# Four 128-column products on four column strips for the last four sections of the modulation

## The chip, the cores and the metric

One core of one Trainium2 chip runs the whole program once. The metric is the device time of one execution in microseconds (us). The engines are named as in the profile: PE is TensorE's matmul side, PEld its weight loads, DVE is VectorE, ACT is ScalarE, POOL is GpSimd, SP is SyncE, which here only issues DMAs.

## What is computed

Two layers share all weights: one for 128 prompt tokens, one for 512 sample tokens, 1024 channels each. Cut to what matters:

```python
mod = silu(cond) @ w_ada + b_ada                      # cond: c_ctx (prompt) or c (sample); 6 x 1024 columns
shift1, scale1, gate1, shift2, scale2, gate2 = split(mod, 6)
h = rms_norm(x) * (1 + scale1) + shift1
P = h @ w_in
mixed = concat(rwkv(P), fnet(P), pool(P))             # rwkv: a delta-rule scan, 8 heads of 64, both directions
x = x + gate1 * (mixed @ w_out)
h = rms_norm(x) * (1 + scale2) + shift2
x = x + gate2 * (relu(h @ w_ff1)**2 @ w_ff2)
y = rms_norm(x)
```

The two condition vectors make the modulation a product of a 2-row matrix with w_ada (1024 x 6144, float32). Sections 0 and 1 (shift1, scale1) are needed before the first projection; sections 2, 4, 3 and 5 (gate1, scale2, shift2, gate2) only behind the mixers.

## The kernel before, in words

All 640 tokens are handled as one [128, 640] row of columns per block of 128 channels. The program runs in three parts.

`first` (line 716) computes the first norm, sections 1 and 0 of the modulation and the projections that the first head pair needs; its order is written out by hand. In it `biasing` (line 813) multiplies the shift with raw blocks of w_in: per block of 128 columns eight products of a [128, 32] stationary operand (`shp`) with 128 moving columns, on the four column strips in turn.

`run_groups` (line 1364) is the part of the mixers. The scan is cut into 24 groups of chunks (4 head pairs, 2 directions, 3 groups each); each group is a generator of stages (products on PE, small masks and copies on DVE, ACT and POOL, at last a chain over the chunks that must follow that of the group before it). At most three groups have a slot. A planner keeps a clock (class `Clock`, line 161) with an estimated cost of each instruction, traces next what comes next by that clock, and `pin` (line 282) makes each compute engine issue in exactly the traced order. Beside the groups there are queues of generators: `preps`, `aux`, `side` and `slow` for background work on the other engines, and `gemms` for products that may fill PE. Lines 1449 to 1457 choose between the next stage of a group and a filler:

```python
a = min(able, key=lambda a: max(a.ready, now + q_.EPS))
gap = a.ready - now
if gap > q_.GAP and gemms and gemms[0].ready <= now + q_.GE:
    gemm_step()          # one step of the first generator of gemms
    continue
if gap > q_.DGAP:
    mm(pm()[:, 0:q_.DN], lm2[:, 0:P], lm2[:, 0:q_.DN], ...)   # a product that nobody reads
```

`gemms` holds first `in_rest` (line 1013, the remaining projections). When that has ended, `second` (line 1560) appends `ada_steps` (line 387) for sections 2, 4, 3, 5, and puts FNet, pooling and `prepare_out` (line 1522, x to channel-major) one behind the other on `slow`. At the end of `prepare_out` the generator `out_half` (line 1505, half of the products with w_out) goes to `gemms`. What is left of all queues is stepped in turn when the last group has ended (line 1476). Then come the rest of w_out, the second norm, the feed-forward and the final norm (lines 1582 to 1730), a dense stream of products with 320 moving columns.

`ada_steps` as `second` uses it handles 512 columns of w_ada at a time, one block of 128 rows a step (`nk` = 1): a DMA on SP brings [128, 1, 512] (256 KB) into one of six slots, three steps ahead (`AH`), and the step issues one product, `sil` [128, 32] stationary (two columns of it are not zero), 512 moving columns, into 32 rows of a PSUM bank: column strip kb % 4 (line 411). Eight steps fill a bank: each strip has the sum over two of the eight row blocks. Then DVE copies the bank (`asb`), four transposes on PE turn it, and DVE adds the four strips and the bias into `mod`. There are 64 product steps and 8 such ends. A float32 product stands in the trace as two matmul records.

Of the kernel before, what the change touches and what calls it, by code (L numbers as in the profile page):

```python
# [13 lines left out]
F32 = mybir.dt.float32  # L14
# [6 lines left out]
P = 128  # L21
D = 1024
# [138 lines left out]
class Clock:  # L161
    """estimate of when each engine and each tile is done with what has been traced; chooses what is traced next"""
# [12 lines left out]
    def cost(self, e, name, out, a, k):  # L175
        n = math.prod(out.shape[1:])
        if e == "P":
            if name == "transpose":
                return 55.0
            x = a[1]  # L180
            if x.dtype != F32:
                return n / 2.4 + (0.5 if x.dtype == F32R else 1.0)
            if out.shape[0] > 64:
                return max(211.0, n / 0.6 + 5.0)
            return 79.0 if n <= 64 else 133.0 * n / 128
        if k.get("op") == ALU.pow:
            return 165.0 * n
        if e == "S" and name == "activation":
            return 145.0 + 0.83 * n
        if e == "V" and name in ("tensor_scalar", "scalar_tensor_tensor") and a[0].space != PSUM and len(a) < 4:  # L190
            return 68.0 + 0.52 * n
        if e == "G" and name != "tensor_tensor":
            return 160.0 + 0.83 * n
        return self.FIXED[e] + self.RATE[e] * n

    def tile(self, x):
        """name of the tile; a new one waits for the last use of the tile whose place it takes"""
        t = x.tensor
        n = t.name
        if n not in self.done:  # L200
            self.done[n] = self.used[n] = 0.0, "P"
            m = getattr(t, "tag_meta", None)
            if m is not None:
                q = self.slots.setdefault(t.cap_key, [])
                q.append(n)
                b = t.bufs or m.bufs
                if len(q) > b:
                    self.done[n] = self.used[q[-1 - b]]
        return n
# [26 lines left out]
class Timed:  # L236
    """an engine whose instructions are noted on the clock"""
# [15 lines left out]
class Task:  # L253
# [4 lines left out]
    def step(self):  # L258
        """one step; it may yield the time that passes before the next, or the tile that the next reads first"""
        c = self.clock  # L260
        c.end = self.ready
        self.state = next(self.gen, "end")
        self.ready = c.end + RD
        if isinstance(self.state, (int, float)):
            self.ready += self.state
        elif hasattr(self.state, "tensor"):
            self.ready = c.done[self.state.tensor.name][0] + RD
        return self.state != "end"


def build(nc, tc, T):
# [10 lines left out]
    def pin(start):  # L282
        """the compute engines issue what was traced since start in the order of the program"""
        prev = {}
        for i in nc.cur_bb.bb.instructions[start:]:
            if i.engine in ENGS:
                if i.engine in prev:
                    tc.add_manual_dep(i, prev[i.engine], mybir.DependencyInfo(mybir.DependencyClass.NoSync, mybir.DependencyReason.DATA),
                                      reason="program order")
                prev[i.engine] = i.name  # L290
# [7 lines left out]
    def pm():  # L298
        return psb.tile([P, 512], F32, tag="b", name="pb")

# [18 lines left out]
    def wsplit(src, c0, hf, lo_eng, raw=None, to=None):  # L319
        """half of the rows of a block of 128 columns"""  # L320
# [9 lines left out]
    def gemm_steps(pss, w, a, kb, first, last, extra=0):  # L330
        """the products of one block of rows, as a generator over the matrix products"""
# [19 lines left out]
    def gemm(src, c0, a, lo_eng, halves=(0, 1), extra=0):  # L351
        """[P, NT] product with a block of 128 columns of the weights: two banks"""
# [32 lines left out]
    mod = cp.tile([P, 48, 2], F32, name="mod")  # L385

    def ada_steps(ks, slots, nk, ahead, queue=None):
        """sections of the modulation: 1024 columns each, 512 at a time; slots name the places of the weights"""
        todo = [(k, h, k2) for k in ks for h in range(2) for k2 in range(KB // nk)]
        place = {}  # L390

        def load(n):
            if queue is None and n < len(todo):
                k, h, k2 = todo[n]
                pool, tag, bufs = slots[n % len(slots)]
                place[n] = pool.tile([P, nk, 512], F32, tag=tag, name="wa", bufs=bufs)
                c0 = k * D + 512 * h
                dma(place[n][:], T["w_ada"][nk * k2 * P:nk * (k2 + 1) * P, c0:c0 + 512].rearrange("(a p) n -> p a n", p=P))

        for n in range(ahead):  # L400
            load(n)
        for n, (k, h, k2) in enumerate(todo):
            load(n + ahead)
            r = place.pop(n) if queue is None else queue.pop(0)
# [11 lines left out]
            yield  # L416
            ps2 = pm()
# [77 lines left out]
    npad = [0]  # L495

    def evac(pss, pp, o=0, b=None):
        """out of the banks, with the bias b, or that of the last two columns; pads between the segments if o is not None"""
# [24 lines left out]
    def proj(pool, pss, mi, out, b=None):  # L523
        """w_in block with centred shift, into out [P, NT]"""
        pp = padded(pool)
        evac(pss, pp, b=b)
        shift_a(mi, pp, out, V)
        shift_b(mi, pp, out, out)
# [13 lines left out]
    def cp(out, ps):  # L542
        """out of PSUM, by the engine that is done with it first"""
# [8 lines left out]
    def mm2(lhsT, rhs):  # L552
        """[P, NT] product in two banks; yields (columns, psum)"""
# [72 lines left out]
    def pool_mix(fp):  # L626
# [12 lines left out]
        for pb in range(2):  # L639
# [6 lines left out]
            def doubling(shape, n, src, sl, tag):  # L646
                """centred window sums along a zero-padded axis: the tiles of half the widest window and of the widest"""
# [46 lines left out]
    def rsq_bcast(sq, op0, s1, op1, s2):  # L694
        """(head sums of sq [P, NT], op0 s1, op1 s2) ** -0.5, spread over the channels of each head: (columns, psum)"""
# [20 lines left out]
    def first():  # L716
        """the first norm, the modulation and the projections that the first groups need"""
        with tc.tile_pool(name="pq", bufs=1) as pq:
# [37 lines left out]
            ada = ada_steps((1, 0), None, 2, 0, wa)  # L756
# [8 lines left out]
            def mids(*plan):  # L765
                """gaps of products, and a step of the modulation behind each"""
# [46 lines left out]
            def biasing():  # L813
                """the products of the shift with the raw weights of the first blocks, as a generator"""
# [44 lines left out]
            def products(n, mid=iter(())):  # L859
                """the n-th half; the weights of the next are split ahead"""  # L860
# [111 lines left out]
    def make_sets(pool, n, tag):  # L972
        """tiles with blocks that stay zero, a set for each slot"""
# [27 lines left out]
    def step(q):  # L1001
        """one step of the first task of a queue"""
# [10 lines left out]
    def in_rest():  # L1013
        """the remaining projections; weights are split half a block ahead of the product"""
# [58 lines left out]
    def prep(c, d, g, pool, out):  # L1073
        """elementwise operands of the chunks of a group"""
# [75 lines left out]
    def group(c, d, g, pool, own, pc, AR, BK):  # L1150
        """chunks g of direction d of a head pair, as a generator over stages"""
# [18 lines left out]
        # ---- Gram blocks, token-major copies  # L1170
# [25 lines left out]
        # ---- inverse of I - T: doubling in 16 bit, one correction step with a float32 residual  # L1196
# [5 lines left out]
        def diag(lhs, rhs, o=0):  # L1202
            """products of the pairs of blocks on the diagonal with the chunks of a pair"""
# [10 lines left out]
        # M V  # L1214
# [49 lines left out]
        # ---- W, Z  # L1264
# [18 lines left out]
        # ---- chain over chunks  # L1283
# [80 lines left out]
    def run_groups(todo):  # L1364
        """todo: (j, g, d) in order; as many in flight as there are slots; the chains of a direction run in order"""
# [24 lines left out]
        while todo or active or prepared or preps:  # L1390
# [17 lines left out]
            # ---- background steps whose operands are there  # L1408
# [96 lines left out]
    def out_half():  # L1505
        """the products of w_out with the channels of the FNet and pooling mixers"""
# [15 lines left out]
    def prepare_out():  # L1522
        """x to channel-major, FNet and pooling outputs split"""
# [36 lines left out]
    def second():  # L1560
        acs.close()
        gemms.append(task(ada_steps((2, 4, 3, 5), [(wp, "whi", WB), (wp, "wlo", WB)], 1, AH)))
# [19 lines left out]
    with tc.tile_pool(name="fc", bufs=1) as fc:  # L1582
# [47 lines left out]
        with tc.tile_pool(name="ffp", bufs=1) as ffp:  # L1630
# [21 lines left out]
            # ---- the last quarter by tokens, and the final norm behind it  # L1652
            with tc.tile_pool(name="op", bufs=2) as op:
# [6 lines left out]
                def part(t, q):  # L1660
                    """half of the channels of a tile of tokens, and the sum of their squares"""
# [108 lines left out]
```

## Time and profile before

| what | value |
|---|---|
| runs of the kernel before | 1136.89, 1140.99, 1140.12 us; median 1140.12 |
| the profiled execution, span from first to last instruction | 1140.2 us |
| mean granted TensorE clock | 0.983 |
| PE busy | 1095.3 us (96%), 9516 instructions |
| DVE, ACT, POOL busy | 544.5, 506.4, 383.3 us |
| modulation products (tile wa) | 192 matmul records, first at 15.4 us, last at 541.4 us |
| DMA of w_ada in the part of the mixers | 64 issues of 256 KB, median 3.2 us to landing |

The page is read from the top: PE is busy nearly all the time, but a busy PE is not a PE at its peak, since a matmul's record covers its latency. The part of the mixers lies between 80 and about 620 us, and there the other engines are busy for half of the time or more; behind it DVE, ACT and POOL fall off and PE runs alone. A start in a row is counted from the start of the span. In the timeline a row merges neighbouring instructions of one kind: its time runs from the first start to the last end, and the next row's start may lie before that end.

### The profile page before, as it was taken

The page shows a single profiled execution, that of the slowest core. Times are in us where ns is not written, and L with a number is a line of the kernel's source. Part 1 is how long each engine was busy: PE and PEld are TensorE (multiplying, and loading weights), DVE is VectorE, ACT ScalarE, POOL GpSimd, SP SyncE. Part 2 cuts the span into 40 slices and gives each one's busy share as a digit, 9 for nine tenths or more (in the row PEclk, how much of TensorE's full clock was granted, in tenths as well). Part 3 has the DMA queues.
Part 4 walks back from the last instruction along what each step waited for, and adds up shares of the span by engine and source line. Part 5 has one row for each costly group of instructions (what it writes and reads, how often), then busy time and mean ns, then how long its engine had stood idle before and what let it go on. Part 6 is the DMA issues. An engine that isn't in the chain of part 4 may idle for free.

```text
span 1140.2 us, 23679 instructions
## 1 busy us (share of the span) xinstructions
PE 1095.3 (96%) x9516; PEld 949.0 (83%) x9516; DVE 544.5 (48%) x1297; ACT 506.4 (44%) x1221; POOL 383.3 (34%) x462
## 2 busy tenths in 40 slices
PE   5999999999999998998999999999999999999996
PEld 3688888788785665565677999999999999999996
DVE  6266665466665654667754664311331233123313
ACT  5243575655565454654762354312431243124412
POOL 4224431124222133464300283333333333333520
PEclk9999999999998999998999999999999999999999
DMA  9522311111313345442313322222222222222212
GB/s 321 184 62 81 94 36 58 51 51 43 95 64 121 112 139 166 124 133 69 111 56 97 117 74 75 75 75 75 75 76 80 76 76 75 75 74 75 77 45 93
DMA packets 130383, 104.11 MB, mean 91 GB/s; under 512 B 9309, under 2 KB 108642, under 8 KB 130274
## 3 DMA queue, kind: packets, MB, share of 16 engines
q1 hardware_dynamic: 114290, 81.22, 23.5%
q10 hardware_dynamic: 15552, 21.05, 6.2%
q8 instruction: 75, 1.23, 0.4%
q0 software_dynamic: 432, 0.33, 0.2%
q14 instruction: 34, 0.28, 0.1%
HBM read 90.52 MB, written 9.76 MB: 88 GB/s over the span
## 4 chain that ended last, share of the span: by engine, by line
PE 82%; issue 6%; DVE 6%; POOL 2%; ACT 1%; DMA 0%; ACTq 0%; DVEq 0%; POOLq 0%
PE pb L248 82%; DVE t L248 1%; DVE EB L248 1%; DVE bda L248 1%; POOL st L248 1%; DVE P L248 1%; DVE hlo L248 0%; DVE BK L248 0%; POOL t L248 0%; DMA wpl<-w_pool 0%; POOL bda L248 0%; ACTq L248 0%; DVE dd L248 0%; DVE W L248 0%; DVE y L248 0%
## 5 line engine op out<-in xcount | busy, mean ns | idle before, releaser
L248 POOL TENSOR_TENSOR wlo<-raw,whi 128x512 fp32r<-128x512 f32 x125 | 162.3, 1299 | 268.5 <-ACT whi L248 266.2
L248 ACT CAST whi<-raw 128x512 fp32r<-128x512 f32 x161 | 99.8, 620 | 276.6 <-PE pb L248 251.0
L248 PE MATMUL pb<-h2l,whi 128*128 128x320 f32 (+1 forms) x512 | 155.4, 310 | 0.0
L248 PE MATMUL pb<-h2h,whi 128*128 128x320 f32 (+1 forms) x512 | 155.3, 311 | 0.0
L248 DVE SCALAR_TENSOR_TENSOR x<-pb,mod,x 128x128 f32<-128x128 f32 (+1 forms) x144 | 55.0, 433 | 172.9 <-PE pb L248 172.7
L248 PE MATMUL pb<-fh,whi 128*128 128x320 f32 (+2 forms) x408 | 123.3, 310 | 0.0
L248 PE MATMUL pb<-fl,whi 128*128 128x320 f32 (+2 forms) x408 | 122.7, 308 | 0.0
L248 PE MATMUL pb<-h2h,wlo 128*128 128x320 f32 (+1 forms) x512 | 117.0, 310 | 0.0
L248 PE MATMUL pb<-hhi,whi 128*128 128x320 f32 (+1 forms) x304 | 99.1, 331 | 0.0
L248 PE MATMUL pb<-hlo,whi 128*128 128x320 f32 (+1 forms) x304 | 98.6, 329 | 0.4 <-DVE hlo L248 0.4
L248 PEld LDWEIGHTS pb<-h2l,whi 128*128 128x128 f32 x512 | 96.6, 189 | 0.0
L248 PEld LDWEIGHTS pb<-h2h,whi 128*128 128x128 f32 x512 | 96.5, 189 | 0.0
L248 PE MATMUL pb<-fh,wlo 128*128 128x320 f32 (+2 forms) x408 | 94.6, 309 | 0.0
L248 PEld LDWEIGHTS pb<-h2h,wlo 128*128 128x128 f32 x512 | 86.3, 188 | 0.0
L248 POOL TENSOR_TENSOR t<-t,k 128x256 f32<-128x256 f32 (+1 forms) x24 | 15.9, 664 | 208.2 <-DVE t L248 197.5
L248 PE MATMUL pb<-hhi,wlo 128*128 128x320 f32 (+1 forms) x304 | 78.8, 328 | 0.0
L248 PEld LDWEIGHTS pb<-fh,whi 128*128 128x128 f32 x408 | 77.1, 189 | 0.0
L248 PEld LDWEIGHTS pb<-fl,whi 128*128 128x128 f32 x408 | 76.3, 187 | 0.0
L248 DVE TENSOR_TENSOR rl<-pb,rs 128x320 f32<-128x320 f32 x64 | 30.3, 486 | 94.3 <-PE pb L248 94.1
L248 PEld LDWEIGHTS <-bda 128*128 128x128 f16 x880 | 43.1, 99 | 37.8 <-issue 13.9
L248 ACT COPY W<-pb 128x256 f32<-128x256 f32 (+3 forms) x144 | 54.4, 398 | 41.5 <-DVE W L248 29.2
L248 PEld LDWEIGHTS pb<-fh,wlo 128*128 128x128 f32 x408 | 68.6, 188 | 0.0
(271 smaller groups left out, 2399.7 us busy)
## 6 DMA issues: line engine op xcount, KB each, us to landing
raw<-w_ff SPq DMA_DIRECT2D x128, 256.0 KB, 2.8
wa<-w_ada SPq DMA_DIRECT2D x64, 256.0 KB, 3.2
wa<-w_ada SPq DMA_DIRECT2D x16, 512.0 KB, 8.7
raw<-w_in SPq DMA_DIRECT2D x30, 256.0 KB, 2.9
raw<-w_out SPq DMA_DIRECT2D x16, 256.0 KB, 2.8
ukd<-shq ACTq DMA_DIRECT2D x9, 320.0 KB, 2.5
ds<-dft_s ACTq DMA_DIRECT2D x8, 257.0 KB, 2.7
x<-x_sample SPq DMA_DIRECT2D x4, 512.0 KB, 5.8
```

The lines of the kernel that those rows point to most:

```text
L248: return fn(out, *a, **k)
```

## The change

`ada_steps` keeps only the form that `first` uses. A new generator `ada_quads` takes its place in `second`. It goes through the same columns in the same eight steps per 512, but a step is now one block of 128 columns and four blocks of rows: the DMA brings [128, 4, 128] (256 KB, runs of 512 bytes instead of 2 KB), and the step issues four products of 128 moving columns, one on each column strip, into the same 128 columns of the bank. The end of a section is the same, but for the yield behind the copy, which names the tile. The planner's cost of a float32 product with 32 output rows changes from 133 ns per 128 columns to 72 ns per 128 columns (430 ns for 512). The diff also takes comments and doc strings out in many places, which is left out here.

```diff
@@ class Clock, cost @@
             if out.shape[0] > 64:
                 return max(211.0, n / 0.6 + 5.0)
+            if out.shape[0] == 32:
+                return 72.0 * n / 128 if n < 512 else 430.0
             return 79.0 if n <= 64 else 133.0 * n / 128
...
-    def ada_steps(ks, slots, nk, ahead, queue=None):
+    def ada_steps(ks, nk, queue):
         todo = [(k, h, k2) for k in ks for h in range(2) for k2 in range(KB // nk)]
...
-            load(n + ahead)
-            r = place.pop(n) if queue is None else queue.pop(0)
+            r = queue.pop(0)
...
+    def ada_quads(ks, slots, ahead):
+        todo = [(k, h, cb, k2) for k in ks for h in range(2) for cb in range(4) for k2 in range(2)]
+        place = {}
+        def load(n):
+            if n < len(todo):
+                k, h, cb, k2 = todo[n]
+                pool, tag, bufs = slots[n % len(slots)]
+                place[n] = pool.tile([P, 4, P], F32, tag=tag, name="wa", bufs=bufs)
+                c0 = k * D + 512 * h + P * cb
+                dma(place[n][:], T["w_ada"][4 * k2 * P:4 * (k2 + 1) * P, c0:c0 + P].rearrange("(a p) n -> p a n", p=P))
+        for n in range(ahead):
+            load(n)
+        for n, (k, h, cb, k2) in enumerate(todo):
+            load(n + ahead)
+            r = place.pop(n)
+            yield r[:]
+            if cb == 0 and k2 == 0:
+                ps = pm()
+            for i in range(4):
+                q = 32 * i
+                mm(ps[q:q + 32, cb * P:(cb + 1) * P], sil[:, 4 * k2 + i, :], r[:, i, :], start=k2 == 0, stop=k2 == 1, tile_position=(0, q))
+            if cb < 3 or k2 == 0:
+                continue
+            asb = wp.tile([P, 512], F32, tag="raw", name="asb", bufs=RB)
+            V.tensor_copy(asb[:], ps[:])
+            yield asb[:]
...
-            ada = ada_steps((1, 0), None, 2, 0, wa)
+            ada = ada_steps((1, 0), 2, wa)
...
-        gemms.append(task(ada_steps((2, 4, 3, 5), [(wp, "whi", WB), (wp, "wlo", WB)], 1, AH)))
+        gemms.append(task(ada_quads((2, 4, 3, 5), [(wp, "whi", WB), (wp, "wlo", WB)], AH)))
```

## Rows read from the trace of the kernel before

**Rows 1.** Stretches: span, length, then each engine's busy time and count, clock, DMA.

```profile
340.00:540.00 200.00, 187.50 (x1963) 119.73 (x1961) 121.68 (x324) 108.83 (x319) 73.07 (x111) 0.96 0.41 123
540.00:590.00 50.00, 47.20 (x686) 37.04 (x684) 33.62 (x84) 35.92 (x93) 13.36 (x17) 1.00 0.30 93
```

**Rows 2.** The chain that ended last: start, length, what, number of instructions.

```profile
358.23 37.88 PE pb L248 x303
...
628.13 503.34 PE pb L248 x3414
```

**Rows 3.** Tile wa: one row of all, its stretch, its share inside seven chain pieces.

```profile
L248 PE MATMUL pb<-wa,sil x192: 589/593/1062, 15.4 to 541.4; 128*32 128x512 f32 x192
...
340.00:560.00 220.00, 39.58 (x128) 5.43 (x128) 0.96 0.41 123
...
sum 102.18, PE 28.01 PEld 3.85; mean PE 4.00 PEld 0.55
```

**Rows 4.** Timeline of PE at a lone product and at four on the strips; DVE between.

```profile
15.44 1.06 PE L248 MATMUL pb<-wa,sil 128*32 128x512 f32 x8
16.44 0.76 PE L248 MATMUL pb<-ident,x 128*128 128x128 f32 x5
...
369.07 1.05 PE L248 MATMUL pb<-wa,sil 128*32 128x512 f32 x2
370.05 0.23 PE L248 MATMUL pb<-P,bda 128*128 128x64 f16 x2
...
369.12 0.49 DVE L248 TENSOR_TENSOR P<-pb,lmask 128x128 f16<-128x128 f32 x2 [0.59 <-PE pb L248]
```

**Rows 5.** Tile shp: its busy time; the timeline of PE around one burst and later.

```profile
59.00:63.00 4.00, 2.58 (x64) 1.50 (x64) 0.00 (x0) 0.00 (x0) 1.00 0.15 42
...
59.08 0.31 PE L248 MATMUL pb<-hhi,whi 128*128 128x320 f32 x1
59.32 0.64 PE L248 MATMUL pb<-w,shp 128*32 128x128 f32 x16
59.89 0.41 PE L248 MATMUL pb<-hlo,whi 128*128 128x320 f32 x1
...
63.04 0.31 PE L248 MATMUL pb<-hhi,whi 128*128 128x320 f32 x1
63.19 0.31 PE L248 MATMUL pb<-hlo,whi 128*128 128x320 f32 x1
```

**Rows 6.** Timeline of PE at a run of products; the chain behind it.

```profile
353.98 1.06 PE L248 MATMUL pb<-wa,sil 128*32 128x512 f32 x8
...
354.71 0.44 DVE P L248
...
355.19 2.54 PE pb L248 x36
```

**Rows 7.** Tile lmask on PE (products that nobody reads), by stretch.

```profile
340.00:540.00 200.00, 9.29 (x29) 0.96 0.41 123
540.00:590.00 50.00, 7.45 (x24) 1.00 0.30 93
```

**Rows 8.** Tile X by stretch: PE, DVE (one a group), ACT.

```profile
97.00:340.00 243.00, 14.63 (x188) 4.45 (x12) 15.14 (x45) 0.99 0.21 64
340.00:584.00 244.00, 12.84 (x192) 4.39 (x12) 16.00 (x47) 0.97 0.39 119
```

**Rows 9.** Issues of DMAs: KB each, median us to landing.

```profile
wa<-w_ada SPq DMA_DIRECT2D x64, 256.0 KB, 3.2
...
raw<-w_in SPq DMA_DIRECT2D x30, 256.0 KB, 2.9
```

**Rows 10.** Transposes of x (tile xq); products of tile mh in the stretch behind them.

```profile
L248 PE MATMUL pb<-ident,xq x40: 272/272/329, 560.5 to 584.2; 128*128 128x128 f32 x40
...
590.00:618.00 28.00, 15.83 (x62) 10.71 (x62) 0.00 (x0) 0.00 (x0) 0.00 (x0) 0.94 0.14 41
```

**Rows 11.** An idle PE in its timeline, and the stretch behind it.

```profile
446.23 3.75 PE L248 MATMUL pb<-EB,oopa 128*128 128x128 f32 x16 [3.85 <-ACT oopa L248]
...
447.00:451.00 4.00, 4.00 (x30) 3.38 (x30) 1.70 (x5) 2.81 (x9) 1.09 (x4) 0.57 0.87 209
```

More of the change, by code (lines that the diff above doesn't have):

```diff
@@ L385, in build @@
     mod = cp.tile([P, 48, 2], F32, name="mod")
-    def ada_steps(ks, slots, nk, ahead, queue=None):
+    def ada_steps(ks, nk, queue):
         todo = [(k, h, k2) for k in ks for h in range(2) for k2 in range(KB // nk)]
[L390 to L401, printed above, removed]
         for n, (k, h, k2) in enumerate(todo):
-            load(n + ahead)
-            r = place.pop(n) if queue is None else queue.pop(0)
+            r = queue.pop(0)
             yield r[:]
@@ L416, in ada_steps @@
             yield
+            ps2 = pm()
+            for i in range(4):
+                PE.transpose(ps2[:, i * P:(i + 1) * P], asb[:, i * P:(i + 1) * P], ident[:])
+            ms = mod[:, 8 * k + 4 * h:8 * k + 4 * h + 4, :]
+            V.tensor_reduce(ms, ps2[:].rearrange("p (n q c) -> p n c q", n=4, q=4)[:, :, 0:2, :], axis=mybir.AxisListType.X, op=ALU.add)
+            V.tensor_tensor(ms, ms, pv("b_ada", 8 * k + 4 * h, 4).unsqueeze(2).broadcast_to([P, 4, 2]), op=ALU.add)
+            yield
+    def ada_quads(ks, slots, ahead):
[16 more added lines that the diff above has]
+                ps = pm()
+            for i in range(4):
+                q = 32 * i
[5 more added lines that the diff above has]
+            yield asb[:]
             ps2 = pm()
```

## The prediction, made before the changed kernel was run

> **What bounds the kernel now.** I read the stretches first, then the chain of waits, then the tiles of the modulation, and last the timeline around single steps. The stretches [rows 1] show the part of the mixers with PE busy for 187.5 of 200 us and DVE and ACT for 122 and 109: no other engine is near its limit, but a busy PE is not a PE at its peak. The chain [rows 2] runs on PE in long pieces here, broken by DVE, ACT and POOL; from 628.13 us on it is one piece of 503 us on PE to the end. So a product of `out_half` that is left over for the end costs its full time, while one that is saved between 340 and 620 us pays only where PE was what the next step waited for. The modulation of sections 2, 4, 3, 5 lies at 340 to 560 us [rows 3]: 128 matmul records, that is 64 products, with PE busy on them for 39.6 us. No group needs them; they are gap fillers. What they cost is how much longer than the gap they are.
>
> **A product before.** A lone one takes PE from 369.07 to 370.05, 0.98 us [rows 4]. Four on four strips took from 15.44 to 16.44, 1.00 us [rows 4]: strips run side by side, and a lone product leaves three of them empty. The planner counts 0.53 us for one (133 ns per 128 columns, line 194), so in a gap that it takes for long enough the product runs over by some 0.45 us.
>
> **A step after.** Its shape is on record: `biasing` issues the same form (128 rows, 32 columns, 128 moving) on strips in turn. Its 64 records are 32 products, eight steps' worth, with PE busy for 2.58 us [rows 5]: 0.32 us a step. One burst of two steps' worth holds PE from 59.32 to 59.89 [rows 5], 0.29 us a step where steps follow each other; that is the lower end, and the 0.57 us of the whole burst the upper one for a step alone. Getting into the burst costs too: 59.08 to 59.32 is 0.24 us where the same products later follow at 0.15 [rows 5]. For a step alone I take 0.35 us, an estimate near the lower end, because the second step's worth in that burst is what the upper end has too much. 64 steps at 0.32 make 20.6 us: PE is freed of 39.6 - 20.6 = 19.0 us.
>
> The Trainium skill (TensorEngine Tiling (Array Packing), Key Properties) says that a change of the tiling mode drains TensorE, which speaks against many small steps: if each of the 64 stood alone, at my 0.35 us they would cost 22.4 us and free 17.2. The 0.24 us before the burst fits that rule, and the forecast hardly moves by it.
>
> **What of the 19 us reaches the end.** First, not all of it was on the path: seven pieces of the chain on PE between 345 and 505 us hold 28.0 of the 39.6 us [rows 3]; cut in the same ratio (20.6 to 39.6), they lose 28.0 x 0.48 = 13.4 us.
>
> Second, a shorter filler uncovers the wait it filled. Behind the lone product at 369.07 PE needs P, which DVE has written by 369.61 [rows 4]; PE starts 0.04 us after such an end (355.15 to 355.19 [rows 6]), so it could go on at 369.65 instead of 370.05: 0.40 of the 0.63 us saved. Behind the run at 353.98, P was ready only at 355.15 [rows 6]: nothing is gained. Where the next product's operands were long there, all of it is. Between nothing and all I take the middle case, 0.40 / 0.63: 13.4 x 0.63 = 8.4 us. What is late next is DVE's mask, P.
>
> Third, `out_half`. It cannot start before the last transposes of x at 584 us [rows 10], which come through FNet, pooling and `prepare_out`, a queue of its own. Behind that it gets 15.8 of 28 us of PE [rows 10], 57%. If the groups end 8.4 us earlier and that queue does not move, 8.4 x 0.57 = 4.8 us of its products move into the stretch where PE is the chain. If it moves as much as the groups (all engines are pinned to one order, so a late PE delays it too) the loss is nothing. I take half: 2.4 us. That leaves 8.4 - 2.4 = 6.0 us.
>
> **Costs that I put at nothing.** The loads: 64 of 256 KB on SP before and after, in runs of 512 bytes instead of 2 KB. Blocks of w_in have the very form of the new ones and land in 2.9 us, against 3.2 for w_ada now [rows 9]; so they are no later, and three steps of lead cover them. If steps are taken faster than loads come, the planner sees no ready filler and puts in a product that nobody reads; it does not wait. The ends of the sections (copy, transposes, sum) are the same work, eight times; the yield that now names the tile asks for the same moment. 192 more products are only issued: the burst shows that this keeps pace. `first` has a hand-written order; its new planned cost shifts the clock before the groups, but all engines start there from one common value.
>
> **The new order** is the cost that no row shows. With 0.29 us planned for a step, the planner deals all groups anew from 340 us on. The nearest rows: twelve groups took 243 us beside the projections and 244 us beside the modulation [rows 8], with quite other fillers in between. So a new deal as such is worth a microsecond either way by these, and I put it at nothing, with 3 us either way in the range.
>
> The sum: the profiled execution has 1140.2 us of span, all but equal to the median of the three runs (1140.12, from 1136.89 to 1140.99). 1140.2 - 6.0 = 1134.2, **1134 us**.
>
> **The rivals.**
> - All of it counts. If the part of the mixers is bound by PE's total work, the planner fits the smaller steps into gaps without loss and the 19.0 us come off: 1121 us. For it: PE at 187.5 of 200 us [rows 1]. Against it: 29 products that nobody reads in 340 to 540 us [rows 7], so gaps were there that had no filler at all.
> - Nothing counts. The pace is set by the latency of the groups, with three in flight, and by their work on DVE, ACT and POOL. For it: the equal pace of 243 and 244 us [rows 8], whatever filled PE. Against it: the long PE pieces of the chain [rows 2], with the modulation inside them [rows 3]. The time would be 1140, between 1137.5 and 1143.
> - Slower: the fillers run out. At about half the length more steps go into each gap, and the 64 can be used up near 440 us instead of 541. From there to the start of `out_half` the gaps hold only products that nobody reads, as in 540 to 590 us, 24 of them in 50 us against 29 in 200 before [rows 7], and where the planner sees no gap PE stands idle. What idle time costs beyond itself: PE stood idle for 3.85 us before 446.23, and in the next 4 us the granted clock was 0.57 [rows 11], most of them at the lower of its two levels, 1.2 GHz: 0.43 x 4 = 1.7 us of PE's time. It decides from four more such falls with nothing gained: 1140.2 + 4 x 1.7 = 1147 us; with a gain of 6 us as forecast they would only cancel it. Against it: in 540 to 590 us the clock stayed at 1.00 [rows 1]. The Trainium skill (TensorE: Matmul & The Clock Gate, What's actually happening) says that the throttled clock is the default and that activity lifts it; by that rule PE's freed time is not free of risk, and the row with 0.57 agrees.
>
> That the strips do not run side by side in this form is no rival: rows 5 show them doing it.
>
> **How the numbers follow.** The forecast, part of the gain, has 0.45, and a range of its own from 1129 (no loss to `out_half`, three of the new order in its favour) to 1138 (the whole loss to it, and the order against it). All of it: 0.15. Nothing: 0.25. Slower: 0.15. Half a per cent, 5.7 us, is about what a measurement of this kernel can tell from no change: faster is below 1134.4, slower above 1145.8. Of the forecast's 0.45 two thirds lie below 1134.4; with the first rival that is 0.45 for faster. The rest of the forecast and the second rival make 0.40 for the same, the last rival 0.15 for slower. The range of 1121 to 1147 takes in the first rival and the price of the last, and leaves out some 0.1 beyond these two.
>
> **What would show it.** Right, step by step: the tile wa with 512 records in the part of the mixers and PE busy on them for 20 to 23 us; a lone step near 0.35 us; the last of them well before 541 us; more than the 53 products that nobody reads of rows 7; the last long PE piece of the chain starting some 6 to 8 us before 628, and being up to 5 us longer than 503. The forecast is wrong if a step alone takes PE over 0.57 us, if that last piece starts where it did (nothing counts), or if it starts 15 us or more earlier (all counts). The last rival would show in more stretches with a granted clock near 0.57 between 440 and 590 us.

## The result, and the profile after

The change makes the kernel slower: 1146.17 us (median of 11 runs, 1138.91 to 1156.79) against 1137.90 us (11 runs, 1136.37 to 1141.69), ratio 1.0059, 95% interval 1.0033 to 1.0086. The longest run counts as slow and is left out of the ratio, which the record gives by itself and which is not the quotient of the two medians. The forecast was 1134, faster or the same; the measured time lies inside the range of 1121 to 1147, at the end that the last rival set. The profiled execution of after took 1152.26 us, more than the median; it has 1150.2 us of span.

The page of after, its first and second part:

```profile
span 1150.2 us, 24461 instructions
...
PE 1094.6 (95%) x9899; PEld 968.6 (84%) x9909; DVE 552.0 (48%) x1297; ACT 505.7 (44%) x1221; POOL 382.1 (33%) x462
...
PEclk8999999999999998897789899999999999999998
```

PE is busy for as long as before (1095.3 us) although its products got shorter, and six of the slices 16 to 23 show a granted clock of 0.7 or 0.8. The mean over the span is 0.965, against 0.983.

The tile wa of after, all of it and its stretch (columns as in [rows 3]):

```profile
L250 PE MATMUL pb<-wa,sil x576: 272/273/1062, 15.5 to 566.7; 128*32 128x128 f32 x170, 128*32 128x512 f32 x22
...
340.00:570.00 230.00, 24.17 (x512) 12.51 (x512) 0.89 0.42 123
```

PE's timeline in after at a lone step and at three:

```profile
369.02 0.43 PE L250 MATMUL pb<-wa,sil 128*32 128x128 f32 x8
369.38 0.23 PE L250 MATMUL pb<-P,bda 128*128 128x64 f16 x2
...
449.94 0.86 PE L250 MATMUL pb<-wa,sil 128*32 128x128 f32 x24
450.73 0.68 PE L250 MATMUL pb<-W,EB 64*64 64x64 f32 x16
```

The lone step at the very place of [rows 4] holds PE from 369.02 to 369.38, 0.36 us instead of 0.98; three behind each other 0.79 us. PE is busy with the 64 steps for 24.17 us instead of 39.58 [rows 3]. But the last of them comes at 566.7 us, not earlier than 541.4 but later.

The stretches of after (first all engines, then tile lmask on PE, then tile X on PE, DVE and ACT), columns as in [rows 1, 7, 8]:

```profile
340.00:540.00 200.00, 176.84 (x2318) 132.55 (x2316) 127.86 (x323) 109.98 (x324) 74.97 (x111) 0.91 0.43 124
540.00:590.00 50.00, 46.31 (x555) 36.05 (x556) 29.41 (x68) 29.06 (x75) 11.37 (x17) 0.81 0.31 93
...
340.00:540.00 200.00, 12.72 (x39) 0.91 0.43 124
540.00:590.00 50.00, 4.41 (x15) 0.81 0.31 93
...
340.00:590.00 250.00, 14.19 (x188) 4.48 (x12) 15.86 (x47) 0.89 0.40 118
```

The last piece of the chain in after:

```profile
656.15 485.32 PE pb L250 x3307
```

PE idles 23.2 of the first 200 us (12.5 before), and the clock there is 0.91 and 0.81 where it was 0.96 and 1.00. The twelve groups took 250 us, not 244 [rows 8]. The last piece of the chain starts 28 us later and is 18 us shorter: 10 us are lost, all of them before it.

**Where the time went.** Both kernels take 467.4 us from the first product of the feed-forward (tile h2h; 672.8 before, 682.8 after) to the end, and both reach the thirteenth group's X at 346.4 us. So the difference lies between these two moments. One row of the stretches, from the one to the other, splits it. Before:

```profile
346.40:672.80 326.40, 305.94 (x3136) 222.50 (x3133) 200.89 (x495) 176.47 (x469) 108.68 (x138) 0.96 0.38 112
```

After:

```profile
346.40:682.80 336.40, 304.94 (x3524) 242.27 (x3527) 208.60 (x495) 176.19 (x469) 108.12 (x138) 0.90 0.37 109
```

PE's idle time is the length less PE's busy time. What the clock withheld is at most the length times one less the clock (two decimals: within 1.7 us). The rest is what the stage would take with PE never idle and at its full clock:

| profiled execution (kernels are told below) | stage | PE idle | withheld | rest |
|---|---|---|---|---|
| before | 326.4 | 20.5 | 13.1 | 292.8 |
| e1: new products, old order | 322.6 | 28.5 | 19.4 | 274.7 |
| e2: old products, new order | 330.6 | 21.4 | 16.5 | 292.7 |
| after | 336.4 | 31.5 | 33.6 | 271.3 |
| e0: the change again | 330.4 | 28.4 | 29.7 | 272.3 |
| e16: before, loads on SP | 319.0 | 16.8 | 9.6 | 292.6 |
| e15: e1, loads on SP | 309.6 | 21.2 | 12.4 | 276.0 |
| e13: after, loads on SP | 316.6 | 25.1 | 15.8 | 275.7 |

The rest is 293 us with the old products and 271 to 276 with the new ones, in whatever order: 16.6 to 21.5 us less, where the forecast had freed PE of 19.0. So the products did free what they should. In after, 11.0 us of that turned into idle time of PE and 20.5 us into lower clock, and so more was given back than won; in e0, whose execution (1146.97 us) lies nearer to the median, it was 7.9 and 16.6 us.

### The profile page after: what moved, and what is told of

Its sections match the earlier page's. It is cut to its first block, busy times and chain, and to the rows that moved or that the text cites. A ratio compares the mean times of both kernels' runs of the same rounds, so it can differ in the third digit from the quotient of the medians.

```text
span 1150.2 us, 24461 instructions
## 1 busy us (share of the span) xinstructions
PE 1094.6 (95%) x9899; PEld 968.6 (84%) x9909; DVE 552.0 (48%) x1297; ACT 505.7 (44%) x1221; POOL 382.1 (33%) x462
## 4 chain that ended last, share of the span: by engine, by line
PE 81%; DVE 6%; issue 5%; DMA 3%; ACT 2%; POOL 1%; ACTq 1%; SPq 0%; DVEq 0%; POOLq 0%
PE pb L250 81%; DVE t L250 1%; DVE bda L250 1%; DMA wa<-w_ada 1%; DVE y L250 1%; ACTq L250 1%; DVE EB L250 0%; DVE sq L250 0%; DMA yc<-ycd 0%; DMA ycd<-px 0%; DVE P L250 0%; POOL st L250 0%; ACT bda L250 0%; DVE BK L250 0%; DMA x<-x_sample 0%
## 5 line engine op out<-in xcount | busy, mean ns | idle before, releaser
L250 POOL TENSOR_TENSOR t<-t,k 128x256 f32<-128x256 f32 (+1 forms) x24 | 15.8, 660 | 207.6 <-DVE t L250 194.4
L250 PEld LDWEIGHTS <-bda 128*128 128x128 f16 x880 | 44.8, 101 | 29.5 <-issue 10.6
```

Of the source, the lines that this page charges most:

```text
L250: return fn(out, *a, **k)
```

## The experiments

Times are medians; a ratio is to the kernel before in runs on the same chip, with its 95% interval. The clock is the median over a kernel's runs.

**Products and order apart.** The diff does two things: shorter products, and a planner's cost that deals all groups anew. e1 takes the second away, e2 the first; e0 is the change again, in the same comparison. In e1 all engines issue in the order of before, in e2 in that of after.

```diff
 e1, on the change, class Clock, cost
-            if out.shape[0] == 32:
-                return 72.0 * n / 128 if n < 512 else 430.0
 e2, on before, class Clock, cost (step32 is 288.0 at a step of second, else None)
+            if out.shape[0] == 32:
+                return self.step32 if n == 512 and self.step32 else 72.0 * n / 128 if n < 512 else 430.0
```

> The products of the change, with the planner's cost of before (four times 133 ns, so 532 ns a step as before): all engines issue in the order of before, only the product steps differ. Theory A (the new order lost the time: its stalls, and the clock falls that follow them): the shorter products pay as forecast, 1130 to 1135 us, granted clock at or above 0.98. Rival B (a PE that has less to do has its clock lowered, whatever the order): the clock goes to 0.97 or less and the time to 1140 to 1148. Rival C (the pace is set by other engines): 1137 to 1141, clock as before.

> The products of before (one of 512 columns a step), but planned at the cost of the change (288 ns a step): all engines issue in the order of the changed kernel. Theory A: the order alone loses what the products gained on top, 1149 to 1157 us, with the stalls of the changed kernel at the same places. Rival B: PE has as much to do as before, so the clock is back at 0.98 and the time at 1138 to 1143. Rival C: 1143 to 1148, as the changed kernel.

> The changed kernel itself, on the chip of this comparison: 1143 to 1149 us by every theory, with a spread of 10 us or more between its runs, and the longer runs at the lower granted clock.

| | us | ratio | clock |
|---|---|---|---|
| before | 1140.36 | | 0.985 |
| e1 | 1137.88 | 0.9985 (0.9965 to 1.0006) | 0.979 |
| e2 | 1151.05 | 1.0100 (1.0079 to 1.0121) | 0.979 |
| e0 | 1148.20 | 1.0068 (1.0042 to 1.0094) | 0.9685 |

The products alone are worth -2.5 us in the old order, where the interval takes in no change, and 1148.20 - 1151.05 = -2.9 us in the new one. The order alone costs 10.7 us with the old products and 10.3 with the new. The two add up; the loss is the order's. e2 came out as its theory A expected. e1 fits none of its three whole: it has the time of C, but a clock 0.006 below that of before.

**Other orders for the same products.** The planned cost of a 128-column product, 72 ns in the change, is set to 89 (e3; the diff) and, alike, to 110 (e8); e1 has 133.

```diff
-                return 72.0 * n / 128 if n < 512 else 430.0
+                return 89.0 * n / 128 if n < 512 else 430.0
```

> The change with 89 ns instead of 72 planned for a product (356 ns a step, what a lone step took in the trace of the changed kernel): another deal of the order from the first step on. Theory A (the order decides, and any deal is a draw): a time that differs from the changed kernel by more than 3 us either way, anywhere from 1130 to 1150. Rival B: the clock stays low, 0.965 to 0.972, and the time within 3 us of the changed kernel.

> The change with 110 ns planned for a product: one more deal of the order with the same products. If the deal is a draw, it lies anywhere from 1135 to 1150 us and not in line between the deals at 72 (1148), 89 (1144) and 133 ns (1138); if the time follows the planned cost, it lies between the last two, 1139 to 1143.

89: 1144.21, ratio 1.0030 (1.0009 to 1.0050), clock 0.973. 110: 1136.63, ratio 0.9969 (0.9953 to 0.9985), clock 0.982. So the same 64 steps give ratios from 0.9969 to 1.0068, some 11 us apart, by the deal alone. A lone step of four took 0.36 us, 90 ns a product, and three steps 0.79, 66 ns; the costs nearest to these, 72 and 89, gave the slower deals. A truer cost did not make a better deal.

**Is it PE's idle time as such?** If PE's clock falls because gaps stay empty, more products that nobody reads should help, and fewer should hurt. e5 (on the change) and e6 (on e1) issue each such product behind the start of the modulation twice, the second one unseen by the planner; e7 cuts them in before to 64 columns at the old planned cost.

```diff
 e5, e6, in run_groups (e7 alike, with one product of 64 columns)
-                mm(pm()[:, 0:q_.DN], lm2[:, 0:P], lm2[:, 0:q_.DN], start=True, stop=True)
+                dum = pm()
+                mm(dum[:, 0:q_.DN], lm2[:, 0:P], lm2[:, 0:q_.DN], start=True, stop=True)
+                if not then:
+                    nc.tensor.matmul(dum[:, 0:q_.DN], lm2[:, 0:P], lm2[:, 0:q_.DN], start=True, stop=True)
```

> The changed kernel with each of its 62 unread products behind the start of the modulation issued twice, about 14 us of PE work more; its order kept. Clock theory: clock from 0.969 to 0.975 or more, time at or below the changed kernel, 1138 to 1147 us. Rival: clock within 0.002 of 0.969, time 1149 to 1160.

> The products of the change in the order of before (the kernel of 1137.9 us at a clock of 0.978), with each of the 53 unread products behind the start of the modulation issued twice, about 12 us of PE work more in the same gaps. Clock theory: clock back to 0.983 or more, time 1131 to 1137, faster than both kernels. Rival: clock within 0.002 of 0.978, time 1138 to 1148.

> The kernel before, with the 53 unread products behind the start of the modulation cut from 512 to 64 columns (about 10 us of PE work less, nothing that anyone reads); the order of all engines as before. Clock theory (less PE work in the gaps lowers the granted clock): clock from 0.985 to 0.978 or less, and the time not shorter, 1139 to 1147 us. Rival (the clock has nothing to do with it, PE work in the gaps is a cost): clock unchanged within 0.002, time 1133 to 1138.

e5: 1155.81, ratio 1.0136 (1.0104 to 1.0168), clock 0.972. e6: 1142.09, 1.0026 (1.0010 to 1.0043), 0.9805. e7: 1140.05, 1.0011 (0.9989 to 1.0032), 0.981. These three ran on another chip than e0 and e1, one where before has a clock of 0.987 instead of 0.985. Set against before, twice the products raise the clock by 0.0015 on the change and lower it by 0.0005 on e1, which shows neither way; shorter ones lower it by 0.006 in e7, as the idle theory says. As a remedy it fails: by the ratios the products cost some 7.7 and 4.7 us. e7 shows the other side: shorter products that nobody reads gain nothing, at a lower clock.

**Why the products paid only 2.5 us.** PE's longest idle time before is 3.85 us before 446.23 [rows 11]; ACT's and POOL's timeline of before shows what stands ahead of it:

```profile
435.87 0.46 ACTq L248 DMA_DIRECT2D ycd<-yf  x1
439.97 0.32 POOL L248 MEMSET wpl<- 128x256 f32 x1 [5.75 <-DVE P L248]
440.31 1.34 ACTq L248 DMA_DIRECT2D wpl<-w_pool  x2
445.59 1.19 ACT L248 COPY oopa<-pb 64x512 f32<-64x512 f32 x2 [8.86 <-DMA px<-fpd]
```

The same of e1:

```profile
434.44 0.41 ACTq L248 DMA_DIRECT2D ycd<-yf  x1
440.09 0.32 POOL L248 MEMSET wpl<- 128x256 f32 x1 [7.00 <-DMA ycd<-yf]
440.44 1.32 ACTq L248 DMA_DIRECT2D wpl<-w_pool  x2
445.57 1.19 ACT L248 COPY oopa<-pb 64x512 f32<-64x512 f32 x2 [10.57 <-DMA px<-fpd]
446.21 1.19 PE L248 MATMUL pb<-EB,oopa 128*128 128x128 f32 x3 [6.93 <-ACT oopa L248]
```

ACT issues FNet's last store, then the loads of pooling. Their tiles take the place of FNet's tiles, so POOL's memset of wpl waits until the store has landed; the loads wait for the memset, and ACT's copy oopa stands behind the loads in ACT's order. PE waits for that copy. How long the store takes to land stands in the view of the DMAs from 430 to 446 us, of before and then of e1:

```profile
ycd<-yf ACTq DMA_DIRECT2D x1, 320.0 KB, 3.9
ycd<-yf ACTq DMA_DIRECT2D x1, 320.0 KB, 5.4
```

So it lands some 0.2 us ahead of the memset in both, though the row of before names DVE. In e1 ACT comes to the store 1.4 us earlier, the store takes 1.5 us longer, ACT waits 1.7 us longer, and the product behind it starts at the same moment, 446.21 and 446.23. That these are equal is chance. Two runs told elsewhere here, e6 and e18, have the products and the order of e1; they come to the store at 432.12 and 431.87 us, and to the product at 443.68 and 443.56. In e18:

```profile
443.56 1.83 PE L248 MATMUL pb<-EB,oopa 128*128 128x128 f32 x6 [6.86 <-ACT oopa L248]
```

What they share with e1 is the landing: 5.4 to 5.5 us in e1, e6, e11 and e18, 3.8 to 3.9 in before, e7 and e12. From the store's issue to the product it takes 11.6 to 11.8 us in e1, e6 and e18 and 10.4 in before, so 1.2 to 1.4 us of what the products had saved until then are lost here. Whether the new loads of w_ada hold the store up was not tested. In the table e1 frees 18.1 us; 8.0 of it come back as idle time of PE, 3.1 of these at this one wait (6.93 us instead of 3.85), and 6.3 as lower clock.

Two edits test what the wait is worth. First, the tiles of pooling get a place of their own (e12 on before, e11 on e1, e10 on the cost of 110, e9 on the change); then SP issues the loads as well, at the same planned time (e16, e15, e14, e13 in that order). The other engines' orders stay.

```diff
 second (e9 to e16)
-            yield from side_pool("fp", fnet)
-            yield from side_pool("fp2", pool_mix)
+            with tc.tile_pool(name="fq", bufs=1, side="right") as fq:
+                yield from side_pool("fp", fnet)
+                yield from side_pool("fp2", lambda fp: pool_mix(fp, fq))
 pool_mix (x and rc alike)
-        wpl = fp.tile([P, 2, P], F32, name="wpl")
+        wpl = fq.tile([P, 2, P], F32, name="wpl")
 pool_mix, e13 to e16 only, at all six loads
-            S.dma_start(x[:], fpd[2 + pb][:])
+            clock.note("A", "dma_start", x[:], (fpd[2 + pb][:],), {})
+            nc.sync.dma_start(x[:], fpd[2 + pb][:])
```

> The same new place in the kernel before, its order kept. There PE was idle for 3.8 us at 442 to 446 us, and the clock fell at 447 us. Theory: 1134 to 1137 us, with the clock up by 0.001 to 0.003. Rival: 1138 to 1141, the wait is taken over by the next one.

> The products of the change in the order of before, with the new place. There PE was idle for 6.9 us before 446 us: the shorter products had only made the wait longer. Theory: that wait goes, 1129 to 1134 us at a clock of 0.981 or more, and against the kernel before with the same new place the products then pay 4 us or more. Rival: 1136 to 1139, and the products pay no more than the 2.5 us seen without it.

> The deal at a planned cost of 110 ns, which was faster than the kernel before by 0.3%, with the new place; PE was idle for 5.8 us before 437 us there. Theory: 1129 to 1133 us, faster than both kernels by 0.5% or more. Rival: 1135 to 1138.

> The changed kernel, with the five tiles that pooling loads first in a place of their own instead of that of FNet's tiles, so that their loads needn't wait until FNet's last store has landed; the order of all engines is kept. In the changed kernel ACT stood behind these loads from 420.7 to 430.6 us and PE was idle for 2.4 and 4.0 us of it. Theory (stalls of the order cost the time twice, as idle PE and as the clock that falls behind them): the idle falls by 3 to 6 us, the clock rises by 0.003 or more, the time falls by 5 to 9 us, to 1139 to 1143 us. Rival (the stall only moves to the next wait): the time stays within 2 us of the changed kernel.

> The same for the kernel before (1140.9 us with the own place alone, PE idle for 4.2 us before 447 us). Theory: 1133 to 1137 us, and the products of the change then pay 4 to 7 us against it in the same order. Rival: 1139 to 1141.

> The same for the products of the change in the order of before (1135.6 us with the own place alone, PE idle for 4.6 us before 441 us). Theory: 1128 to 1132 us. Rival: 1134 to 1137.

> The same for the deal at a planned cost of 110 ns, which took 1131.7 us with the own place alone. Theory: 1126 to 1130 us. Rival: 1131 to 1134.

> The changed kernel with pooling's first tiles in a place of their own and their six loads issued by SP instead of ACT; the compute engines keep the order of the changed kernel. ACT no longer stands for 8 to 10 us near 420 us. Theory (this stall is a large part of the order's loss): PE's idle near 424 to 432 us goes (4 to 6 us), the fall of the clock behind it too, 1134 to 1139 us. Rival (the loss is spread over many small waits and falls): 1141 to 1145 us, clock still at or below 0.972.

| order and products | own place, ratio | and SP's loads, ratio | clock of the latter |
|---|---|---|---|
| before | e12: 1140.90, 1.0018 (1.0004 to 1.0033) | e16: 1133.23, 0.9952 (0.9935 to 0.9968) | 0.990 |
| new products, old order | e11: 1135.59, 0.9979 (0.9961 to 0.9996) | e15: 1125.92, 0.9892 (0.9872 to 0.9913) | 0.983 |
| new products, cost 110 | e10: 1131.70, 0.9942 (0.9921 to 0.9963) | e14: 1128.27, 0.9914 (0.9885 to 0.9943) | 0.9835 |
| the change | e9: 1143.67, 1.0052 (1.0030 to 1.0074) | e13: 1135.96, 0.9974 (0.9951 to 0.9997) | 0.974 |

A place of its own pays only at the cost of 110, as expected there; e9, e11 and e12 came out above what their theories expected. ACT is still held by its six issues: in e11 they run from 432.55 to 440.78 us, and the copy behind them waits 8.22 us, but the product comes at 441.45. With the loads on SP the wait is gone, as e15's timeline shows:

```profile
430.12 1.50 SPq L652 DMA_DIRECT2D wpl<-w_pool  x2
431.19 0.34 ACTq L248 DMA_DIRECT2D ycd<-yf  x1
432.64 1.17 ACT L248 COPY oopa<-pb 64x512 f32<-64x512 f32 x2 [0.91 <-PE pb L248]
435.86 1.95 PE L248 MATMUL pb<-EB,oopa 128*128 128x128 f32 x16
```

In e16 that product comes at 439.11, so now the saved time arrives: 3.3 us by this point. The products are worth 1133.23 - 1125.92 = 7.3 us there, clear of noise, with the 6.0 forecast between that and 2.5. e15 is the best of all, 1.1% below before and 1.8% below the change. The order still costs 1135.96 - 1125.92 = 10.0 us, so the ACT stall is not what the order loses by. e13's time is what its theory expected, but the theory, that the stall is a large part of the order's loss, is not borne out: against e0 and e1 the ratio falls by 0.0094 in the new order (e13) and by 0.0093 in the old (e15).

**What the order loses by.** With the new products it is for the most part the clock: 0.9685 against 0.979 (e0, e1), 0.974 against 0.983 (e13, e15). Within the runs of one kernel a straight line falls 7.3 us for each 0.01 of clock (29 runs of before), 7.4 (e13), 8.9 (e1) and 11.3 (e0, without its longest run), so 0.009 to 0.0105 goes with 7 to 12 of the 10 us. The other kernels lie between 1.8 (e8) and 10.2 (e14), and such a line does not tell what the clock causes from what comes along with it. With the old products it is less: 0.006 (before, e2), 4 to 5 of 10.7 us; where the rest lies is open. In the table of the stage the order's 13.8 us (after against e1) are 14.2 of clock and 3.0 of idle time, less 3.4 of rest. e0 against e1 has 7.8 us: 10.3 of clock, no more idle time, 2.4 less of rest. Between e13 and e15, 7.0 are 3.9 of idle time and 3.4 of clock; e13's profiled execution is one of five at 1130 to 1132 us, while the other seven took 1135 to 1141.

One place was tried. In after DVE, POOL and PE show this (timeline):

```profile
471.77 3.73 DVE L250 TENSOR_TENSOR bda<-EB,i 64x128 f16<-64x128 f32 x2
472.01 3.33 POOL L250 TENSOR_TENSOR ra<-ra 128x1472 f32<-128x1472 f32 x1
476.01 1.33 PE L250 MATMUL pb<-W 64*64 64x128 f32 x10 [2.96 <-DVE W L250]
```

A bda operation of DVE takes 3.28 us beside POOL's long addition and ends just behind it; no bda took over 1.21 us in before or e1. From 475 us on the clock is at its lower level for 6.8 us. e17 (on the change) and e18 (on e1) issue that addition and its like in pieces of at most 6 rows of 64 columns, 384 in all, planned as one.

```diff
-                    (G if EPL else V).tensor_tensor(sl(cur, lo, hi), sl(prev, lo - l, hi - l), sl(prev, lo + r, hi + r), op=ALU.add)
+                    if tag == "ra":
+                        o, a0, a1 = sl(cur, lo, hi), sl(prev, lo - l, hi - l), sl(prev, lo + r, hi + r)
+                        clock.note("G", "tensor_tensor", o, (a0, a1), dict(op=ALU.add))
+                        for i in range(0, hi - lo, 6):
+                            c = slice(i, min(i + 6, hi - lo))
+                            nc.gpsimd.tensor_tensor(o[:, c, :], a0[:, c, :], a1[:, c, :], op=ALU.add)
+                    else:
...
```

> The six additions of pooling's tile ra on POOL are issued in pieces of at most 384 columns, counted by the planner as one as before, so that the order of all engines stays that of the change. In the change a bda operation of DVE takes 3.28 us beside the piece of 1472 columns and PE stands idle for 2.96 us before 476.01, where the granted clock then falls for 6.8 us. If this meeting is one of the places where the new order loses, DVE's operation is over within about 1 us, PE's idle time there is about 1 us or less, and the run is 2 us (the wait alone) to 5 us (the fall too, half of 6.8 us) below the change's, at a ratio of 1.001 to 1.004. If the new order's loss lies in what comes after whatever happens here, the wait shrinks and the ratio stays at 1.005 to 1.008.

> The same pieces on the change's products in the old order, as a control: there no bda operation takes over 1.21 us, so nothing is to be won. If the meeting of DVE and POOL belongs to the new order, this run stays within 1.5 us of the one with the old order (ratio 0.997 to 1.000). If smaller pieces on POOL help in any order, it is 2 us or more below it (ratio under 0.997).

The timeline of e17:

```profile
470.79 1.45 DVE L250 TENSOR_TENSOR bda<-EB,i 64x128 f16<-64x128 f32 x2
471.04 3.82 POOL L693 TENSOR_TENSOR ra<-ra 128x384 f32<-128x384 f32 x4
472.75 1.09 PE L250 MATMUL pb<-W 64*64 64x128 f32 x16 [0.69 <-DVE W L250]
```

PE's wait shrinks from 2.96 to 0.69 us, but the time does not: 1146.55, ratio 1.0077 (1.0049 to 1.0106), clock 0.968; e18 1139.07, 0.9999 (0.9981 to 1.0017), clock 0.977. The meeting is the order's, and it is not what the order loses by. In e17 another 1.44 us of idle time stands before 476.5, and the clock falls at 478.

So no single place of the loss was found. In after the clock falls ten times between 350 and 640 us, for 65 us in all, each time within 4 us of one of 14 idle times of PE of 0.7 to 4.0 us; before it falls five times, for 27 us, with ten such idle times. e0 and e1 are closer: seven falls each, for 55 and 41 us, with 14 and 12 idle times of 0.7 us or more. That the idle times bring the falls fits e7; it is not shown one by one, since idle times of the same length are followed by a fall in one execution and not in the next. Why this deal stalls PE more often, and why the clock is lower by so much, stays open.

## Why the prediction was wrong

- **The step that failed** is "The new order", put at nothing with 3 us either way. It costs 7 to 11 us, by five pairs of kernels (10.7, 10.3, 10.0, by e9 and e11 1143.67 - 1135.59 = 8.1, by e17 and e18 1146.55 - 1139.07 = 7.5). Its evidence was the equal pace of 243 and 244 us [rows 8]. That showed two stretches of one deal; it could not show how far another deal falls off. In after the same twelve groups take 250 us. In e0 the pace of the groups is even that of before, 235.4 us from the thirteenth X to the last (before 236.6), but the feed-forward starts 95.0 us behind the last X instead of 89.8: an equal pace does not bound what a deal costs. What the runs showed in its place is, with the new products, for the most part a lower clock (0.9685 against 0.979, e0 and e1), whose cause is open.
- **The products**: a lone step at 0.35 us measured 0.36. (The planner's 133 ns stand in line 185, not 194.) PE's busy time on them fell by 15.4 us, not 19.0; of the 24.17 us some two belong to the lower clock of this execution (e1 has 21.9 us, e15 21.6). Only 21 of the 64 steps stand alone in after. A step behind another costs 0.21 us more ((0.79 - 0.36) / 2), so some 0.15 us of a lone one are the price of entering. That agrees with the Trainium skill (TensorEngine Tiling (Array Packing), Key Properties), by which a change of the tiling mode drains TensorE; no run separates the drain from other costs of a first product. The rest in the table, 16.6 to 21.5 us less, stands on both sides of the forecast's 19.0.
- **What reaches the end**, 6.0 us, was mis-sized: 2.5 measured in the old order as it stands. The sum had no term for the clock, which took back 6.3 of e1's 18.1 us. The "middle case" of the uncovered waits took each wait by itself. The one at 446 us hangs on a chain off PE (a landing, then six issues on ACT) that grew by 1.2 to 1.4 us with the new products. [Rows 11] showed the wait, and the prediction used it for the clock alone. With that wait gone the same step is worth 7.3 us.
- **`out_half`**: a loss of 2.4 of 8.4 us. In e15 against e16 the stage up to the feed-forward, which holds all of `out_half`, is 9.4 us shorter, with no sign of that loss; its transposes of x come 5.3 us earlier there (569.8 against 575.1 us for the last), so that queue moves too. In the kernel as it stands e1 has them 2.5 us earlier (581.7 against 584.2).
- **Costs put at nothing**: loads land in a median 3.7 us instead of 3.2 [rows 9], so they are later, against the reading of the rows; still the view of tile wa in after lists no idle time of PE ahead of a step in 340 to 570 us. FNet's store, in the same queue of ACT as pooling's loads, was not thought of: it takes 1.5 us longer to land with the new products.
- **The rivals**: "nothing counts" cannot be told from e1's time (0.9985, 0.9965 to 1.0006), but it is not a fixed pace: what was freed went into idle time and clock, and without the ACT stall 7.3 us arrive. The slower rival named the right currency, the clock, and the wrong mechanism: the fillers did not run out (the last step came at 566.7 us, 15 products that nobody reads in 540 to 590 us instead of 24), and the falls lie along the whole stage. Its chance of 0.15 was too small, since it was given to one mechanism, and the order's cost had a range but no sign.

## What to carry to other kernels

A planner's cost model is part of the kernel: a change of a cost is a change of order, and is to be tried apart from the operation that it prices; here the order alone was worth some 11 us (1.0068 against 0.9969), more than the operation was. Before pricing a saving on the busiest engine, look behind it for the next event whose length does not depend on that engine (a DMA's landing, an in-order queue of issues on an engine that also computes): part of what was saved can be lost there, and moving it (here six loads from ACT to SP, and a place of their own) may be worth more than the saving. Where PE is nearly the bound, freed time that turns into short stalls can be paid for twice, as idle time and in the granted clock.

## What was not expected of the hardware

- The clock goes with more than the change is worth: executions of the one kernel e0 ran from 1141.1 us at a clock of 0.974 to 1156.5 us at 0.961.
- The same store of 320 KB, in the same order of all engines, landed in 3.8 to 3.9 us beside the old loads of w_ada (three executions) and in 5.4 to 5.5 us beside the new ones (four).
- A DMA issue on ACT holds ACT's computing in order: with only the six issues of pooling's loads, and what these wait for, between two of its operations ACT stood for 8.2 us (e11) and 10.6 us (e1).
- A 64x128 operation of DVE with both inputs in SBUF took 3.28 us beside an addition of POOL of 3.33 us, and ended just behind it; with the addition in pieces the longest took 1.77 us. The Trainium skill (SBUF — State Buffer, Who interferes with whom) says that such a DVE instruction contends with a GpSimd instruction that reads SBUF, over a shared port pair that it calls an exclusive lock. Both traces agree.
